# Router logits from unscaled rows, the first gather between products, and another layout of the expert blocks

## The chip, the core and the metric

The kernel runs on one core of one Trainium2 chip. The metric is the time of one execution in device microseconds (us). A profiled execution gives the trace from which rows are shown; its engines are TensorE (PE, with its weight loads as PEld), VectorE (DVE), ScalarE (ACT), GpSimd (POOL) and SyncE (SP), which issues most DMA transfers.

## The reference, cut to what matters

A block of a model over 256 tokens of width 1024. First a mixer (retention and dilated attention, conditioned by adaptive shift and scale), then a mixture of experts over 32 experts, then two more blocks (gMLP or block attention, memory heads, feed-forward). The change lies at the passage from the mixer to the experts:

```python
x = x + gt_a[:, None, :] * (merged @ w_o[l])
h = modulate(rms_norm(x, g_ffn[l]), sh_f, sc_f)     # rms_norm(x)*g*(1+sc) + sh
x = x + gt_f[:, None, :] * moe(h, w_router[l], b_router[l], w_mlp1[l], b_mlp1[l], w_mlp2[l], b_mlp2[l])

# moe: top 4 of 32 experts for each token
logits = (xf @ w_router + b_router).astype(jnp.float32)
top_val, top_idx = lax.top_k(logits, TOP_K)
gates = jax.nn.softmax(top_val, axis=-1)
# each expert: u = xb @ w1[e] + b1[e]; clamped SwiGLU; a @ w2[e] + b2[e], weighted by the gate and added up
```

## The kernel before, in words

One core, all 256 tokens in two row blocks of 128 (`tb`). Weights come through a class `Weights`: a plan lists every weight block in the order of use, `load_next` issues the next DMA on SP, and a block is issued only when the buffer that it goes to has been read by all users of its last content. `in_turn` keeps the issues in the order of the plan.

Up to the expert stage, blocks of 1 MB (`raw`, six buffers) are split by ACT and DVE into a high and a low part (`parts`), and each product is three PE products. The last of these is the output projection `wo` in two column halves (`gemm_nat`, L358 to L392; the branch `wo` of the loop at L825 to L847). Behind each half DVE adds the residual into `x`, ACT squares it with a running sum for the norm, and DVE multiplies by the scale `late["ss"][:, 1]` into `h2`.

Then the routing (L874 to L939), at high priority. For each row block: `rsqrt` by Newton steps on DVE; `h2` is scaled by it and the shift `late["ss"][:, 0]` is added (L897, two halves); eight PE transposes, copied by ACT into `h2T`; 8 products with the router's weights give logits with experts on partitions (L909); ACT adds the bias, PE transposes back (L914). Then DVE's top-8 search, the choice matrix `oh` and its sum `pick` (L916 to L921); three products with a triangular and an all-one matrix give each token's rank in its expert (L923 to L925), `R` (L928). Gates `G`, the overflow flag `novi` (L944 to L951) and the transposed gates `GT` (L958) follow. A copy `h2c` of the scaled rows stays for the gather.

The gather of a pair of experts (L986 to L998): a matrix `ohg` that compares ranks with slot numbers (DVE), and 16 products that pick and transpose the rows of `h2c` into `hg` (64 slots per expert), in four quarters `d0`, each emptied by an ACT copy. All four quarters of pair 0 stand ahead of the first chunk.

The expert stage runs over `jobs`: `chunk(p)` (first weights of pair p, u in four PSUM banks, transposed back, SwiGLU into `apk`) and `second(p)` (second weights, the spread back to tokens), in the order c0, c1, h0, c2, h1, ... Each of the 16 first weights of a chunk is one plan entry of 1 MB; two are loaded by one 2 MB DMA into a turning place. There are eight places, taken in turn: `big0` to `big5` in the pool `upper`, where `raw` and `parts` were, `middle` and `lower` below it. Entries 12 to 15, used in the last quarter of chunk 0, are one-off 1 MB blocks in places of the lasting pool `pa`: x1, x2, reth, retl. The place x1 holds `u` (`us_`) afterwards. `chunk` also issues the next pair's gather, a quarter ahead of each quarter of its own products. The instructions of each engine run in the order that the scheduler fixes from priorities and a simulated time.

After the last pair the turning places are given back, and buffers for the next stage open there, with a place `kvp` for keys and values of the memory heads.

## Time and profile before

| | us |
|---|---|
| median of three timed runs | 1926.49 |
| lowest and highest | 1925.88, 1928.82 |
| profiled execution | 1928.28 |
| its span, first to last instruction | 1926.6 |
| PE busy | 1841.6 (96%) |
| DVE busy | 803.5 (42%) |
| ACT busy | 536.6 (28%) |

The mean granted clock of TensorE is 0.984. A busy time is a count over the whole span and says little of one stage; the rows below are of the passage and of the stage behind it. In a timeline a row can merge several instructions of one kind: start, length from the first start to the last end, and their number behind the x; the brackets give idle time ahead of the first and what ended it. Matmuls are pipelined, so that the ends of neighbours overlap. A float32 product appears as two instructions, a transpose as one.

### The profile page before, as it was taken

What the parts mean: (1) busy time and instruction counts of PE and PEld (TensorE: products, weight loads), DVE (VectorE), ACT (ScalarE), POOL (GpSimd) and SP (SyncE); (2) the same over time, 40 slices, a digit from 0 to 9 for tenths busy, and PEclk for the clock granted to TensorE, in tenths of its full rate; (3) what the DMA queues carried; (4) which work ended last, traced back from release to release, by engine and by line L of the source; (5) the groups of instructions that cost most, each with busy time, mean ns of one, the idle gap of its engine ahead of it and who ended that gap; (6) DMA issues with size and microseconds to landing.
All of it is one profiled execution on the core that took longest, in us unless ns stands there. A gap on an engine that the chain in (4) does not pass through costs nothing. (4 is left out here: it accounts for less than half of the span.)

```text
span 1926.6 us, 23931 instructions
## 1 busy us (share of the span) xinstructions
PE 1841.6 (96%) x10132; PEld 1212.7 (63%) x10132; DVE 803.5 (42%) x1283; ACT 536.6 (28%) x792; POOL 2.6 (0%) x7
## 2 busy tenths in 40 slices
PE   7999999899999999998999899899999999999998
PEld 6899987543344434333333344238889998879997
DVE  5787477422221212221112212028564457565445
ACT  3545454210000000000000000005544445645443
POOL 0000000000000000000000000000000000000000
PEclk9999999999999999999999999999999999999999
DMA  9777476999999999999999999998455555326550
GB/s 359 254 261 249 151 257 229 372 404 416 427 426 427 427 427 427 426 428 427 427 427 427 427 426 427 424 370 294 142 180 190 179 193 176 111 97 225 181 175 23
DMA packets 160403, 593.05 MB, mean 308 GB/s; under 512 B 7643, under 2 KB 92214, under 8 KB 134690
## 3 DMA queue, kind: packets, MB, share of 16 engines
q1 hardware_dynamic: 154008, 583.25, 77.4%
q10 hardware_dynamic: 6282, 8.21, 1.4%
q8 instruction: 81, 1.33, 0.3%
q14 instruction: 32, 0.26, 0.0%
HBM read 590.37 MB, written 1.07 MB: 307 GB/s over the span
## 5 line engine op out<-in xcount | busy, mean ns | idle before, releaser
L1028 PE MATMUL bank_a<-big,hg 128*64 128x512 f32 x2016 | 478.3, 604 | 17.0 <-DMA big<-in_w_mlp 16.9
L197 DVE TENSOR_TENSOR wlo<-raw,whi 128x1024 fp32r<-128x1024 f32 x286 | 345.4, 1222 | 252.7 <-ACT whi L196 251.7
L196 ACT ACTIVATE whi<-raw 128x1024 fp32r<-128x1024 f32 x286 | 298.2, 1058 | 346.9 <-issue 101.0
L1028 PEld LDWEIGHTS bank_a<-big,hg 128*64 128x64 f32 x2016 | 146.5, 139 | 304.1 <-issue 269.4
L1028 PE MATMUL bank_b<-big,apk 128*64 128x512 f32 x928 | 223.6, 617 | 20.7 <-DMA big<-in_w_mlp 20.7
L400 PE MATMUL bank_b<-xh,wlo 128*128 128x256 f32 x640 | 181.1, 283 | 0.0
L398 PE MATMUL bank_b<-xh,whi 128*128 128x256 f32 x640 | 181.1, 283 | 0.0
L399 PE MATMUL bank_b<-xl,whi 128*128 128x256 f32 x640 | 181.0, 283 | 0.0
L1028 PEld LDWEIGHTS bank_b<-big,apk 128*64 128x64 f32 x928 | 84.1, 141 | 148.5 <-issue 93.4
L1050 DVE COPY us<-bank_a 128x512 f32<-128x512 f32 x32 | 22.1, 692 | 345.9 <-PE bank_a L1028 345.9
L398 PEld LDWEIGHTS bank_b<-xh,whi 128*128 128x128 f32 x640 | 122.7, 192 | 0.7
L399 PEld LDWEIGHTS bank_b<-xl,whi 128*128 128x128 f32 x640 | 122.6, 192 | 0.7
L400 PEld LDWEIGHTS bank_b<-xh,wlo 128*128 128x128 f32 x640 | 122.7, 192 | 0.0
L352 ACT ACTIVATE us<-bank_a 128x512 f32<-128x512 f32 x32 | 19.1, 597 | 328.9 <-PE bank_a L1028 328.9
L1086 DVE TENSOR_TENSOR y<-bank_b,gtf 128x512 f32<-128x512 f32 x32 | 22.1, 692 | 201.6 <-PE bank_b L1028 200.1
L352 ACT ACTIVATE spread<-bank_b 128x256 f32<-128x256 f32 x16 | 6.1, 384 | 299.2 <-PE bank_b L1096 299.2
L997 PEld LDWEIGHTS bank_b<-ohg,h2c 128*128 128x128 f32 x512 | 66.1, 203 | 23.0 <-issue 21.1
L997 PE MATMUL bank_b<-ohg,h2c 128*128 128x128 f32 x512 | 72.7, 294 | 0.0
L1499 PE MATMUL bank_a<-wlo,ah 128*128 128x512 f32 x176 | 69.8, 396 | 0.0
L1500 PE MATMUL bank_a<-whi,al 128*128 128x512 f32 x176 | 69.7, 396 | 0.0
L1498 PE MATMUL bank_a<-whi,ah 128*128 128x512 f32 x176 | 69.7, 396 | 0.0
L352 ACT ACTIVATE hg<-bank_b 128x256 f32<-128x256 f32 x64 | 24.6, 384 | 149.2 <-PE bank_b L997 149.2
(382 smaller groups left out, 2735.2 us busy)
## 6 DMA issues: line engine op xcount, KB each, us to landing
big<-in_w_mlp SPq DMA_DIRECT2D x184, 2048.0 KB, 27.0
raw<-in_w_ffn_in SPq DMA_DIRECT2D x44, 1024.0 KB, 5.1
raw<-in_w_in SPq DMA_DIRECT2D x38, 1024.0 KB, 7.5
raw<-in_w_ada SPq DMA_DIRECT2D x24, 1024.0 KB, 6.6
raw<-in_w_ffn_out SPq DMA_DIRECT2D x22, 1024.0 KB, 4.9
raw<-in_w_mlp SPq DMA_DIRECT2D x16, 1024.0 KB, 14.7
raw<-in_b_w_in SPq DMA_DIRECT2D x10, 1024.0 KB, 5.2
raw<-in_w_mix_out SPq DMA_DIRECT2D x8, 1024.0 KB, 5.2
```

Of the source, the lines that this page charges most:

```text
L196: self.nc.scalar.activation(hi, w, AF.Copy)
L197: self.nc.vector.tensor_tensor(lo, w, hi.bitcast(F32), OP.subtract)
L352: return S.activation(o, i, AF.Copy, **kw)
L398: PE.matmul(v[:, m], hi[:, k, ms], xh[:, k], start=k == 0, stop=False)
L399: PE.matmul(v[:, m], hi[:, k, ms], xl[:, k], start=False, stop=False)
L400: PE.matmul(v[:, m], lo[:, k, ms], xh[:, k], start=False, stop=k == 7)
L997: PE.matmul(b[:, n], h2c[:, tb, c0:c0 + 255:2], ohs[p_][:, tb], start=tb == 0, stop=tb == 1)
L1028: last[:] = [PE.matmul(out[at], st, w, start=start, stop=stop)]
L1050: V.tensor_copy(us[:, c + 1], u[c + 1])
L1498: PE.matmul(ops[tb, h], ah[:, k, ts], hi[:, k, hs], start=n + k == 0, stop=False)
L1499: PE.matmul(ops[tb, h], ah[:, k, ts], lo[:, k, hs], start=False, stop=False)
L1500: PE.matmul(ops[tb, h], al[:, k, ts], hi[:, k, hs], start=False, stop=n + k == 11)
```

## The change

- The router's logits are taken from rows that carry only the factor `late["ss"][:, 1]`, not the norm and not the shift. The norm `rs` multiplies the logits afterwards (one DVE instruction with the bias), tokens on partitions. The shift's part of the logits is put into the bias ahead: 16 one-row transposes of the shift into columns `shc`, and 8 products, at the head of the branch `wo`. The gathered rows get the shift when `hg` is written (ACT for pair 0, DVE for the others).
- Three of four transposes' groups and the first row block's products stand directly behind the projection's last product (`latest`); the rest behind these. The second norm waits for the first block's `pick`. The comparison matrix of pair 0 is one instruction behind `R`, and the gates wait for it.
- Of pair 0's gather one quarter stands ahead of chunk 0, the others between its products; the gather of pair 1 stands behind each quarter's products. Overflow, gate transposes, biases and spread of pair 0 come after chunk 0.
- Blocks: eight turning places, now `mid` in the lasting pool, six in `upper`, one in `lower`. One-off blocks in reth, retl, x2 and x1 (entries 12 to 15 in this order; 12, 13 and the first 2 MB into `mid` can be asked for ahead of `upper`). The last two turning entries are loaded alone.
- The lasting `mid` holds qT, kT, eT and g_ffn pieces before, kv, gv and junk after the experts. Shift and scale move from reth to x1. The expert biases load on POOL's queue.

```diff
@@ load_next
-        if i in self.doubles:
+        if i in self.doubles or i in self.lone:
...
+            if i in self.lone:
+                self.load(i, t)
@@ load_free
-                h, size, n = (self.history["big"], 2, len(self.bigs)) if i in self.doubles else \
-                    (self.history["raw"], 1, self.nraw)
-                if len(h) >= n and h[-n] + size > self.taken:
+                h, n = (self.history["big"], len(self.bigs)) if i in self.doubles | self.lone else \
+                    (self.history["raw"], self.nraw)
+                if len(h) >= n and h[-n] + (2 if h[-n] in self.doubles else 1) > self.taken:
@@ ada_late_step
-            late["ss"] = pa.tile([P, 2, D], F32, name="ss", tag="reth")
+            late["ss"] = pa.tile([P, 2, D], F32, name="ss", tag="x1")
@@ branch wo, h == 0
+                wr = small(P, 8, 32)
+                nc.scalar.dma_start(wr, A["w_router"][0].rearrange("(k p) e -> p k e", p=P))
+                br = small(P, 32)
+                nc.scalar.dma_start(br, A["b_router"].to_broadcast([P, 32]))
+                shc = keep.tile([P, 2, 8], F32, name="shc")
+                b = bank("b")
+                for k in range(8):
+                    PE.transpose(b[:, k:k + 1], late["ss"][:1, 0, k * P:(k + 1) * P], ident[:1, :1])
+                    d0 = k // 2 * 256 + k % 2
+                    PE.transpose(b[:, 8 + k:9 + k], late["ss"][:1, 0, d0:d0 + 255:2], ident[:1, :1])
+                copy_s(shc.rearrange("p a k -> p (a k)"), b[:, :16])
+                b = bank("b")
+                for k in range(8):
+                    PE.matmul(b[:, :32], shc[:, 0, k:k + 1].to_broadcast([P, P]), wr[:, k], start=k == 0, stop=k == 7)
+                V.tensor_tensor(br, br, b[:, :32], OP.add)
@@ expert blocks
-    W.bigs = [(upper, f"big{i}") for i in range(6)]
-    W.load_early(first_b + 12, pa.tile([P, 2048], F32, name="raw", tag="x1"))
-    W.load_early(first_b + 13, pa.tile([P, 2048], F32, name="raw", tag="x2"))
-    for _ in range(6):
+    W.bigs = [(pa, "mid")] + [(upper, f"big{i}") for i in range(6)]
+    W.lone = {first_b + 370, first_b + 371}
+    W.load_early(first_b + 12, pa.tile([P, 2048], F32, name="raw", tag="reth"))
+    W.load_early(first_b + 13, pa.tile([P, 2048], F32, name="raw", tag="retl"))
+    W.load_next()
+    W.load_early(first_b + 14, pa.tile([P, 2048], F32, name="raw", tag="x2"))
+    for _ in range(5):
         W.load_next()
...
-    W.bigs += [(middle, "big6"), (lower, "big7")]
+    W.bigs.append((lower, "big6"))
+    W.load_early(first_b + 15, pa.tile([P, 2048], F32, name="raw", tag="x1"))
@@ routing
-            scaled = V.scalar_tensor_tensor(h2[:, tb, hs], h2[:, tb, hs], rs, late["ss"][:, 0, hs], OP.mult, OP.add)
...
+        with after(latest[0]):
+            for tb, h in ((0, 0), (0, 1), (1, 0)):
+                blocks(tb, h)
+            dotted = dots(0)
+        with after(dotted):
+            copied = blocks(1, 1)
+            dots(1)
+        for tb in range(2):
+            if tb:
+                with after(picked):
+                    rs.append(rsqrt(ss2[:, 1, 1:], 1.0 / D, ss2[:, 1, :1], 1))
+            V.scalar_tensor_tensor(lg[:, tb], lts[tb][:, :32], rs[tb], br, OP.mult, OP.add)
...
+        routed = V.tensor_tensor(ohs[0], con("slots")[:, None, None, :SLOTS].to_broadcast([P, 2, 2, SLOTS]),
+                                 R[:, :, :2, None].to_broadcast([P, 2, 2, SLOTS]), OP.is_equal)
+        with after(copied):
+            for tb in range(2):
+                copy_s(h2c[:, tb], h2[:, tb], scale=rs[tb])
+    with after(routed):
+        V.tensor_tensor(gates, mx[:, :, :4], mx[:, :, :1].to_broadcast([P, 2, 4]), OP.subtract)
@@ gather
-        copy_s(hg[:, p_ % 2, :, d0:d0 + 2], b.rearrange("p d e s -> p e d s"))
+        if p_ == 0:
+            for n in range(2):
+                S.activation(hg[:, 0, :, d0 + n], b[:, n], AF.Identity, bias=shc[:, 1, d0 + n:d0 + n + 1])
+            return
+        V.tensor_tensor(hg[:, p_ % 2, :, d0:d0 + 2].rearrange("p e d s -> p d e s"), b,
+                        shc[:, 1, d0:d0 + 2, None, None].to_broadcast([P, 2, 2, SLOTS]), OP.add)
-        for d in range(0, 8, 2):
-            gather(0, d)
+        gather(0, 0)
@@ chunk
-            if ahead is not None:
+            if p_ == 0 and k < 6:
+                gather(0, k + 2)
+            if ahead is not None and p_:
                 gather(ahead, k)
...
+            if p_ == 0:
+                with after(*last):
+                    gather(ahead, k)
@@ jobs
-            spread_pair(p_)
+            if p_:
+                spread_pair(p_)
             chunk(p_, p_ + 1 if p_ < 15 else None)
+            if p_ == 0:
+                overflow()
+                spread_pair(p_)
@@ behind the experts
-    kv = kv_[0]
+    mid = pa.tile([P, 4096], F32, name="kv", tag="mid")
+    kv = mid[:, :2048].rearrange("p (n i b t) -> p n i b t", n=2, i=2, b=2)
```

## Rows read from the trace of the kernel before

**Rows 1.** Page, part 2 (GB/s in 40 slices) and part 6 (us to landing).
```profile
GB/s 359 254 261 249 151 257 229 372 404 416 427 426 427 427 427 427 426 428 427 427 427 427 427 426 427 424 370 294 142 180 190 179 193 176 111 97 225 181 175 23
...
big<-in_w_mlp SPq DMA_DIRECT2D x184, 2048.0 KB, 27.0
```

**Rows 2.** Windows, expert stage: PE, PEld, DVE, ACT, POOL busy (count), clock, DMA share, GB/s.
```profile
600.00:800.00 200.00, 189.77 (x862) 79.09 (x860) 41.68 (x72) 14.78 (x27) 0.00 (x0) 0.97 1.01 427
```

**Rows 3.** Windows with the two holes of the stream.
```profile
412.00:414.00 2.00, 2.00 (x13) 0.58 (x8) 0.61 (x1) 0.00 (x0) 0.00 (x0) 1.00 0.70 295
414.00:416.00 2.00, 2.00 (x12) 1.15 (x9) 0.00 (x0) 0.00 (x0) 0.00 (x0) 1.00 0.72 156
...
470.00:480.00 10.00, 10.00 (x54) 4.85 (x52) 0.99 (x5) 0.77 (x2) 0.00 (x0) 1.00 0.96 375
```

**Rows 4.** Timeline: SP's expert loads, and DVE's last reading of the g_ffn piece.
```profile
306.35 19.32 SPq L133 DMA_DIRECT2D raw<-in_w_mlp  x2
...
316.88 0.69 DVE L630 SCALAR_TENSOR_TENSOR ss<-ss,gff 128x512 f32<-128x512 f32 x1 [0.99 <-ACT ss L352]
...
328.82 10.75 SPq L133 DMA_DIRECT2D big<-in_w_mlp  x3
...
359.24 0.42 SPq L133 DMA_DIRECT2D big<-in_w_mlp  x1
...
377.08 222.92 SPq L133 DMA_DIRECT2D big<-in_w_mlp  x47
...
390.82 24.55 SPq L133 DMA_DIRECT2D big<-in_w_mlp  x4
```

**Rows 5.** Timeline of PE, from the projection's end to the first chunk.
```profile
350.06 1.29 PE L900 MATMUL bank_b<-cm,h 128*128 128x128 f32 x8
351.37 1.94 PE L909 MATMUL bank_b<-h2T,rt 128*32 128x128 f32 x16
...
362.99 0.61 PE L958 MATMUL bank_b<-cm,G 128*32 128x128 f32 x2
363.44 6.60 PE L997 MATMUL bank_b<-ohg,h2c 128*128 128x128 f32 x32
```

**Rows 6.** Windows of the projection.
```profile
320.00:325.00 5.00, 5.00 (x24) 4.14 (x23) 2.19 (x2) 2.50 (x3) 0.00 (x0) 1.00 0.01 2
325.00:330.00 5.00, 4.18 (x27) 3.40 (x26) 4.99 (x8) 2.22 (x4) 0.00 (x0) 1.00 0.68 223
```

**Rows 7.** Timeline of DVE in the routing, second row block.
```profile
352.69 0.21 DVE L431 TENSOR_SCALAR rs_z<-rt 128x1 f32<-128x1 f32 x1
...
354.09 1.41 DVE L897 SCALAR_TENSOR_TENSOR h<-h,rs_y,ss 128x512 f32<-128x512 f32 x2
...
359.52 0.20 DVE L916 MAX8 rt<-bank_b 128x8 f32<-128x32 f32 x1 [0.51 <-PE bank_b L914]
...
360.60 0.37 DVE L921 TENSOR_REDUCE rt<-rt 128x32 f32<-128x128 f32 x1
...
361.69 0.22 DVE L928 SCALAR_TENSOR_TENSOR R<-bank_b,rt 128x64 f32<-128x64 f32 x1
...
363.10 0.49 DVE L991 TENSOR_TENSOR ohg<-cm,R 128x128 f32<-128x128 f32 x2
```

**Rows 8.** Timeline at the turn from the first chunk to the second.
```profile
390.62 7.04 PE L1028 MATMUL bank_a<-raw,hg 128*64 128x512 f32 x32
...
395.16 0.60 ACT L352 ACTIVATE us<-bank_a 128x512 f32<-128x512 f32 x1 [24.70 <-PE bank_a L1028]
...
398.89 3.93 PE L997 MATMUL bank_b<-ohg,h2c 128*128 128x128 f32 x32
```

**Rows 9.** Windows of one us: busy of PE first, granted clock third from the end.
```profile
362.00:363.00 1.00, 0.13 (x3) 0.10 (x3) 0.93 (x5) 0.00 (x0) 0.00 (x0) 0.68 1.06 442
...
365.00:366.00 1.00, 1.00 (x7) 1.00 (x7) 0.00 (x0) 0.02 (x1) 0.00 (x0) 0.50 0.99 426
...
369.00:370.00 1.00, 1.00 (x10) 0.88 (x9) 0.00 (x0) 0.35 (x1) 0.00 (x0) 0.90 1.07 459
```

More of the change, by code (lines that the diff above doesn't have):

```diff
@@ L721, in body @@
     pt = ea.enter_context(tc.tile_pool(name="pt", bufs=1, reuse_waits="tile"))
+    mid = pa.tile([P, 4096], F32, name="mid", tag="mid")
+    eTs = [mid[:, 1024 + i * 384:1024 + (i + 1) * 384] for i in range(2)]
     M = {}
@@ L795, in gate, with small @@
         return s_
+    rt, rt_used = None, [4]
+    def small(p, *shape):
+        n = int(np.prod(shape))
+        v = rt[:p, rt_used[0]:rt_used[0] + n]
+        rt_used[0] += n
+        if len(shape) == 2:
+            v = v.rearrange("p (a b) -> p a b", a=shape[0])
+        if len(shape) == 3:
+            v = v.rearrange("p (a b c) -> p a b c", a=shape[0], b=shape[1])
+        return v
     for st_ in stage:
@@ L883, in body, with blocks @@
     ixf = small(P, 2, 8)
+    lg = small(P, 2, 32)
     oh = small(P, 2, 4, 32)
     pick = small(P, 2, 32)
+    ohs = {0: keep.tile([P, 2, 2, SLOTS], F32, name="ohg0", tag="GT")}
     ones = con("ones")
-    hi_prio = ExitStack()
-    hi_prio.enter_context(tc.high_priority())
-    with after(late["sq", 1]):
-        S.activation(small(P, 1), ss2[:, 0, :1], AF.Exp)
+    G = keep.tile([P, 2, 32], F32, name="G")
+    R = keep.tile([P, 2, 32], F32, name="R")
     tss = [slice(0, P), slice(P, T)]
-    copied = None
-    for tb in range(2):
-        rs = rsqrt(ss2[:, tb, 1:], 1.0 / D, ss2[:, tb, :1], 1)
-        for h in range(2):
-            hs = slice(h * 512, h * 512 + 512)
-            scaled = V.scalar_tensor_tensor(h2[:, tb, hs], h2[:, tb, hs], rs, late["ss"][:, 0, hs], OP.mult, OP.add)
+    with tc.high_priority():
+        S.activation(small(P, 1), late["sq0"], AF.Exp)
+        rs = [rsqrt(ss2[:, 0, 1:], 1.0 / D, ss2[:, 0, :1], 1)]
+        lts = [bank("a") for _ in range(2)]
+        def blocks(tb, h):
             b = bank("b").rearrange("p (k t) -> p k t", k=4)
@@ L900, in body @@
                 PE.transpose(b[:, k], h2[:, tb, (4 * h + k) * P:(4 * h + k + 1) * P], ident)
-            c_ = copy_s(h2T[:, 4 * h:4 * h + 4, tss[tb]], b)
-            copied = copied if h else c_
-        if tb:
-            for t_, after_ in ((0, (late["sq", 1], scaled)), (1, (scaled, copied))):
-                with after(*after_):
-                    copy_s(h2c[:, t_], h2[:, t_])
-        lt = bank("b")
-        for k in range(8):
-            PE.matmul(lt[:32, :P], wr[:, k], h2T[:, k, tss[tb]], start=k == 0, stop=k == 7)
@@ L922, in body @@
-    rb = bank("b")
-    PE.matmul(rb[:, :32], con("before"), pick[:, 0], start=True, stop=True)
-    PE.matmul(rb[:, 32:64], ones, pick[:, 0], start=True, stop=False)
-    PE.matmul(rb[:, 32:64], con("before"), pick[:, 1], start=False, stop=True)
-    G = keep.tile([P, 2, 32], F32, name="G")
-    R = keep.tile([P, 2, 32], F32, name="R")
-    V.scalar_tensor_tensor(R, rb[:, :64].rearrange("p (b e) -> p b e", b=2), 1.0, pick, OP.add, OP.mult)
-    dump("h2", h2)
-    gates = small(P, 2, 4)
-    V.tensor_tensor(gates, mx[:, :, :4], mx[:, :, :1].to_broadcast([P, 2, 4]), OP.subtract)
@@ L932, in body @@
-    exped = S.activation(gates, gates, AF.Exp)
-    gl = small(P, 2)
-    V.reduce_sum(gl, gates, AX.X)
-    V.reciprocal(gl, gl)
-    V.tensor_tensor(gates, gates, gl[:, :, None].to_broadcast([P, 2, 4]), OP.mult)
-    for tb in range(2):
-        V.tensor_tensor(oh[:, tb], oh[:, tb], gates[:, tb, :, None].to_broadcast([P, 4, 32]), OP.mult)
-        V.reduce_sum(G[:, tb], oh[:, tb].rearrange("p k e -> p e k"), AX.X)
-    hi_prio.close()
+            return copy_s(h2T[:, 4 * h:4 * h + 4, tss[tb]], b)
@@ new lines, in body @@
+        rb = bank("b")
+        PE.matmul(rb[:, :32], con("before"), pick[:, 0], start=True, stop=True)
+        PE.matmul(rb[:, 32:64], ones, pick[:, 0], start=True, stop=False)
+        PE.matmul(rb[:, 32:64], con("before"), pick[:, 1], start=False, stop=True)
+        V.scalar_tensor_tensor(R, rb[:, :64].rearrange("p (b e) -> p b e", b=2), 1.0, pick, OP.add, OP.mult)
+        routed = V.tensor_tensor(ohs[0], con("slots")[:, None, None, :SLOTS].to_broadcast([P, 2, 2, SLOTS]),
+                                 R[:, :, :2, None].to_broadcast([P, 2, 2, SLOTS]), OP.is_equal)
@@ L983, in body @@
     us_ = pa.tile([P, 4, 512], F32, name="us", tag="x1")
-    spread, ohs = {}, {}
+    spread = {}
     def gather(p_, d0):
-        if d0 == 0:
+        if d0 == 0 and p_:
             ohs[p_] = pe.tile([P, 2, 2, SLOTS], F32, name="ohg")
@@ L1266, in body @@
         nc.gpsimd.memset(q, 0.0)
-    junk = pc.tile([P, D], mybir.dt.bfloat16, name="junk")
+    junk = mid[:, 3584:].bitcast(mybir.dt.bfloat16)
     def normalize(dst, src, st, n, gb):
```

135 lines of the change are left out of this document (63 added, 72 removed).

## The prediction

> **What bounds the kernel now.** I read the slices of the page first: from about 380 to 1250 us the core moves 404 to 428 GB/s and nothing else in the page is as flat [rows 1]. The windows of that stretch say the same more sharply: DMA share 1.01 at 427 GB/s, while PE counts 190 of 200 us [rows 2]. This stage streams 184 blocks of 2048 KB [rows 1] and, by the plan, 16 of 1024 KB of expert weights, 402.7 MB, which at 427 GB/s is 943 us. Whatever moves the end of this stage must move the start of the stream or close a hole in it.
>
> So I looked for holes. There are two behind the start: 412 to 416 us, where the rate falls to 295 and 156, and a small one around 470 to 480 at 375 [rows 3]. In bytes the first is (427-295) x 2 + (427-156) x 2, about 0.8 MB or 1.9 us, the second (427-375) x 10 = 0.5 MB or 1.2 us. The queue's own timeline shows why: two blocks are asked for at 390.82, and the next not before about 414 (the last two of the four that the row merges), since their buffers come free only when the second chunk's first products are through [rows 4]. Products of the first chunk's last quarter free no turning place, because they read the four one-off blocks. Thus **the stream's place after 414 us is set by PE**, not by how early the first blocks were asked for. From the gather at 363.44 on, PE is without a gap, up to beyond that release and through the next one near 474 [rows 3, 5]. After that DMA is the later of the two and stays so. Ahead of 350 us PE is full as well: the output projection runs at 5.00 of 5.00 us per window, with one hole of 0.82 us in 325 to 330 [rows 6]. Between them lies the only stretch in which PE waits: the routing, from 350.0 to 363.4, and after it a gather that runs at half clock.
>
> The forecast is therefore one sum along PE: from the end of the projection to the second chunk's first release, plus what is added ahead of it.
>
> **Part by part.**
>
> *Earlier blocks (reth, retl, mid, x2 ahead of the upper pool; scale and shift in x1).* Today one 1 MB block is asked for at 306.35 and the next about 19 us later, behind the attention buffer; the first 2 MB block follows at 328.82 [rows 4]. After the change two blocks have a free place at 306, the 2 MB one in the lasting pool when the g_ffn piece is read (317.6, the end of L630 [rows 4]), and x2's at 325 as now. That is 5 MB ahead of the upper pool in place of 2: 3 MB, or 7.4 us of stream. But the eight turning places and four one-off blocks still hold 20 MB, and the fifteenth turning block still waits for the second chunk's first products. The lead is spent as a longer hole before 414 us. I count it as 0; its upper worth, 7.4 us, is a rival. On SP's queue these loads stand behind the projection's weights and ahead of expert weights alone. The last two single blocks and the new overlay at the stage's end delay a few 1 MB requests by one quarter chunk (about 7 us) while four to five blocks (27.0 us from issue to landing [rows 1]) are queued: 0. The memories that move into the lasting pool (qT, kT, eT, kv, gv, junk) keep their readers and writers in the same order: 0, with up to 1 us either way.
>
> *Shift columns, new work ahead of the projection.* 16 transposes of a one-row strip, one copy, 8 products (two instructions each, as the sixteen of L909 are for eight) and one add. PE has no cover here but the 0.82 us hole. Price of the transposes, from the nearest rows: at most that of full 128 x 128 ones, eight in 1.29 us, 0.16 each, 2.6 in all; at least a third of that, 0.9, as strips are small. The 16 product instructions: 1.94 us [rows 5]. Sum 2.8 to 4.5, less the hole: **+2.0 to +3.7**, or at best 0, if the order finds more holes. I take +2.7. The Trainium skill ("TensorE: Matmul & The Clock Gate", Part 2, step-by-step) says that loading the stationary operand takes time by its columns and not by its rows, which speaks against the change: a strip of one row by 128 columns would cost what a full block does, and the sum would be +3.7 in place of +2.7. No row here shows a one-row load.
>
> *The routing chain.* Before, from the last product of the projection (350.0, where L900 begins) to the first gather product (363.44): 13.4 us [rows 5]. In it the second row block waits for its own scale (L431 at 352.69) before two scalings of 1.41 us at 354.09; then four transposes and copies, the products, a bias on ACT, a transpose back, and the top-4 chain from 359.52 [rows 7]. After: the unscaled rows need neither scale nor shift, so 12 transposes can start at 350.0 (1.5 us), 8 products of the first row block end near +3.5, the last 4 transposes and the copy follow, and the second block's logits are in PSUM near +6.0. On DVE the first block's chain (L916 to L921, 1.45 us, and a new 0.25 us scaling) ends near +5.3; then, by the order written out, the second scale (1.4, from L431 to L897) at +6.7; then 0.25 + 1.45 again to +8.4; from there to R as now, 0.72 (360.97 to 361.69), and R itself 0.22, to +9.3; one comparison of 128 x 256 in place of two of 128 x 128 (0.49 together), now directly behind R instead of 1.4 us later behind gates and overflow [rows 7]. First gather near **+9.9**: -3.5 us. Waits added: the comparison no longer queues behind the gate arithmetic, which now waits for it; nobody needs the gates before the first chunk ends. The two row copies h2c wait for the second scale on ACT and are through ahead of the gather.
>
> *Gather between products.* The gather of the first pair is 32 instructions: 6.60 us ahead of the first product, at half clock [rows 5], against 3.93 at full clock later [rows 8]. Now one quarter stands ahead and the rest, with the next pair's, between the products. PE does the same instructions on the same gapless path, so moving them gains nothing by itself: the half clock then falls on products instead. From the row, the clock is 0.68 in 362 to 363, 0.50 after that and 0.90 in 369 to 370, after PE had been busy for 0.13 us of a whole one [rows 9]: 6.6 us at half speed, some 3 us lost. After the change the quiet stretch before the gather is 4 us again. I take the same loss, with -2.9 (no fall) to +1.7 (half clock for 10 us) as ends, and lean by -0.4, as the quiet is shorter by one half microsecond.
>
> *Work that comes out of the shadow.* The overflow count and the gate transposes (L958 alone is 0.61 us of PE [rows 5]) stood inside the chain's waits; now they follow the first chunk: +0.6. The biases go from SP's queue to POOL's, where nothing else is queued for hundreds of us; on SP three issues vanish after 359.24 with nothing behind them until 377.08 [rows 4]: 0. Gathers emptied by DVE instead of ACT: neither is near its bound in that stage: 0.
>
> *The turn between the chunks.* The x1 block is now the last of the four one-off blocks and is read by the very last product of the first chunk; the copy of u goes to x1. Today it starts at 395.16, 2.5 us before the last products end (390.62 + 7.04 = 397.66) [rows 8]. After, it starts at the end. PE then has the bias transposes, overflow and spread (about 2.1 us) and the second chunk's products to do. I take +0.3, with 0 to 4.5 as ends.
>
> Sum: +2.7 - 3.5 - 0.4 + 0.6 + 0.3 = -0.3 us; with the small leaning of the memory moves left at 0, **-0.3 us**. The profiled execution took 1928.28 us (span 1926.6), which gives 1928.0. The median of the three timed runs is 1926.49, 1.8 lower, so on the timed scale **1926.2 us**.
>
> **Rivals.**
> - *The clock stays up or the strips are hidden.* With PE busy through more of the chain, the clock need not fall: -2.9; with the strips in holes of the order, -2.7 more. Either alone stays within 4 us, both give 1926.2 - 5.6 = 1920.6; together with half of one, about 1922. For: PE's quiet is shorter than now. Against: 4 us of it remain, and no holes are seen before 350. The Trainium skill ("TensorE: Matmul & The Clock Gate", Part 1) says that the throttled state is the default and activity releases it; the rows agree [rows 9], and no run here shows yet what this quiet does.
> - *The lead of 3 MB reaches the end.* If the second chunk's release came 7 us earlier, the stream would keep its lead: 1926.2 - 7.4 = 1918.8. Against: the release is PE's, by the sum above.
> - *Slower: the turn.* If PE's order leaves the transposes of u at the head while the copies, which start 2.5 us later, and DVE's four additions run one after the other (in the row they are spread over 6 us with products between), PE loses up to 4.5 us before the second release: 1926.2 + 4.2 = 1930.4, and beyond with the full price of the strips (1931.4). It decides from some 4 us of stall on.
> - *The change doesn't do what it says.* If the scheduler puts the whole gather ahead of the products as now, PE's total is the same, and the time too: 1926.
>
> **How the numbers follow.** What a measurement of this kernel can tell from no change is about 0.2%, 3.9 us. Forecast (within 3.9 us of before): 0.54; the turn: 0.16; clock and strips: 0.17; the lead: 0.08; the scheduler's undoing: 0.05, same time. Faster by over 0.2%: 0.17 + 0.08 = 0.25. Same: 0.54 + 0.05 = 0.59. Slower: 0.16. Range: 1921.0 to 1931.0, leaving out the lead and the ends of the rivals beyond it.
>
> **What would show it.** In the changed profile: two 1 MB and one 2 MB expert block asked for before 320 us; the hole of DMA before the second chunk's release near 414 grown from 2 to about 9 us; the projection's end moved from 350.0 to about 352.7; first gather about 10 us behind that; the second chunk's first release within 3 us of 414. If that release moves by more than 4 us, the forecast is wrong by as much, and the step is the one whose row moved: strips, chain, clock or turn. If it doesn't move but the time does, the cause lies behind 1300 us, in a place I set at 0.

## The result, and where the profile after differs

The changed kernel took 1942.55 us (median of 4 runs, 1939.38 to 1947.76) against 1927.65 for the kernel before on the same chip: a ratio of 1.0079, 95% interval 1.0066 to 1.0092. It is **slower by 0.8%**, 11.6 us above the upper end of the forecast's range. The profiled execution took 1939.72 us (span 1938.0 against 1926.6), one of the two faster of its four; the other two took 1945 and 1948.

Where 11.3 us arise, as far as one trace of each kernel tells, is read from how much later the same event comes in the trace after than in the trace before:

| event | before, us | after, us | shift | gained or lost since the row above |
|---|---|---|---|---|
| last 1 MB block of `w_o` asked for | 305.89 | 309.18 | +3.3 | +3.3 |
| first product of the output projection | 326.99 | 337.93 | +10.9 | +7.6 |
| its last product ends | 349.99 | 360.89 | +10.9 | 0 |
| first gather | 363.44 | 371.94 | +8.5 | -2.4 |
| 25th block of 2 MB asked for | 456.73 | 466.52 | +9.8 | +1.3 |
| last expert product ends | 1297.70 | 1309.12 | +11.4 | +1.6 |
| first block of `w_ffn_in` asked for | 1357.4 | 1370.9 | +13.5 | +2.1 |
| last product of PE | 1918.28 | 1929.59 | +11.3 | -2.2 |

The largest loss lies where I had put +2.7: ahead of the projection. The first product is no like mark in the two traces: before, six products stand between the first eight of the 16 transposes of `m1` (the rows that the projection reads) and the next, and PE waits 0.82 us there; after, all 16 come first. The projection's end is a like mark, and gives the same +7.6 since the `w_o` block. The timeline of PE after (start, duration, engine, line), answering [rows 5]:

```profile
329.51 0.22 PE L856 MATMUL bank_b<-cm,ss 1*128 1x1 f32 x1
...
330.85 0.25 PE L858 MATMUL bank_b<-cm,ss 1*128 1x1 f32 x1
331.38 3.43 PE L862 MATMUL bank_b<-rt,shc 128*128 128x32 f32 x16 [0.27 <-ACT shc L356]
334.62 3.65 PE L565 MATMUL bank_b<-cm,m 128*128 128x128 f32 x16
337.93 0.71 PE L370 MATMUL bank_a<-whi,hh 128*128 128x512 f32 x1
...
360.73 1.47 PE L923 MATMUL bank_b<-cm,h 128*128 128x128 f32 x12
362.04 2.84 PE L928 MATMUL bank_a<-rt,h2T 128*128 128x32 f32 x24
...
366.74 1.89 PE L928 MATMUL bank_a<-rt,h2T 128*128 128x32 f32 x8
...
371.94 3.75 PE L1027 MATMUL bank_b<-ohg,h2c 128*128 128x128 f32 x16 [0.87 <-DVE rt L961]
```

The 16 one-row transposes are cheap, 1.6 us; the 16 product instructions behind them (L862) take 3.43 us, where 24 of the same shape take 2.84 at 362.04 (the 16 of [rows 5], 1.94, from which I had the price, have another shape), and then the 16 transposes of `m1` (L565), older work, take 3.65. The windows of this stretch (busy of PE, PEld, DVE, ACT, POOL, then granted clock, DMA share, GB/s) say why: 0.50 is 1.2 GHz, and PE has no pause in it. In [rows 6] all is at 2.4.

```profile
330.00:332.00 2.00, 1.73 (x17) 1.64 (x16) 2.00 (x4) 0.91 (x2) 0.00 (x0) 0.90 0.71 172
332.00:338.00 6.00, 6.00 (x31) 6.00 (x30) 2.27 (x4) 1.74 (x3) 0.00 (x0) 0.50 1.00 374
338.00:340.00 2.00, 2.00 (x10) 1.64 (x9) 1.38 (x2) 0.66 (x2) 0.00 (x0) 0.89 1.00 426
```

SP's expert loads, answering [rows 4], came as the diff says: two at 309.64 (before: one), the 2 MB one of `mid` at 321.59. The second chunk's first release went from 414.20 to 421.50, and the hole ahead of it grew as forecast (198 and 291 GB/s below, 329 and 431 before):

```profile
309.64 1.07 SPq L133 DMA_DIRECT2D raw<-in_w_mlp  x2
321.59 0.33 SPq L133 DMA_DIRECT2D big<-in_w_mlp  x1
...
421.50 10.97 SPq L133 DMA_DIRECT2D big<-in_w_mlp  x4
```

```profile
410.00:420.00 10.00, 10.00 (x58) 4.91 (x58) 5.12 (x11) 2.15 (x4) 0.00 (x0) 1.00 0.47 198
420.00:430.00 10.00, 10.00 (x50) 3.89 (x47) 2.66 (x8) 1.91 (x3) 0.00 (x0) 1.00 0.77 291
```

Three smaller losses stood at 0 or nowhere in my sum: +3.3 ahead of 306 us, +1.6 at the end of the expert stage, +2.1 behind it; and the last stage runs *faster* than before.

### The profile page after: what moved, and what is told of

Its sections match the earlier page's. It is cut to its first block, busy times and chain, and to the rows that moved or that the text cites. A ratio compares the mean times of both kernels' runs of the same rounds, so it can differ in the third digit from the quotient of the medians.

```text
span 1938.0 us, 23994 instructions
## 1 busy us (share of the span) xinstructions
PE 1846.8 (95%) x10162; PEld 1212.1 (63%) x10162; DVE 824.7 (43%) x1341; ACT 514.8 (27%) x735; POOL 4.2 (0%) x10
## 5 line engine op out<-in xcount | busy, mean ns | idle before, releaser
L1055 PE MATMUL bank_b<-big,apk 128*64 128x512 f32 x928 | 219.0, 606 | 20.0 <-DMA big<-in_w_mlp 20.0
L1055 PEld LDWEIGHTS bank_b<-big,apk 128*64 128x64 f32 x928 | 78.3, 139 | 149.1 <-issue 100.7
L1032 DVE TENSOR_TENSOR hg<-bank_b,shc 128x256 f32<-128x256 f32 x60 | 25.4, 423 | 103.6 <-PE bank_b L1027 103.6
```

What stands on the lines that cost most here:

```text
L1032: V.tensor_tensor(hg[:, p_ % 2, :, d0:d0 + 2].rearrange("p e d s -> p d e s"), b, shc[:, 1, d0:d0 + 2, None, None].to_broadcast([P, 2, 2, ...
L1055: last[:] = [PE.matmul(out[at], st, w, start=start, stop=stop)]
```

## Experiments

Sixteen kernels. Where an expectation speaks of the eighth, eleventh or fourteenth experiment, it counts otherwise than here: they are 10, 6 and 12. Shifts are against the trace before. One thing blurs them: near 50 us the clock falls for longer in some executions than in others, which moves all that follows by up to 4 us (at 60 us the traces lie between -1.8 and +4.3 of the one before). The same window in the trace before, and in that of the fourteenth kernel, which has the same work there (clock third from the end):

```profile
50.00:55.00 5.00, 5.00 (x17) 3.28 (x17) 4.88 (x7) 5.00 (x8) 0.00 (x0) 0.82 1.04 385
```

```profile
50.00:55.00 5.00, 5.00 (x11) 2.71 (x11) 4.77 (x11) 4.41 (x7) 0.00 (x0) 0.50 1.04 385
```

So I read differences of shifts within a trace, and medians for whole times; a median of five or six executions can still hold more of the one kind than of the other.

### The strips

**1. Without strips.**

```diff
-                for k in range(8):
-                    PE.transpose(b[:, k:k + 1], late["ss"][:1, 0, k * P:(k + 1) * P], ident[:1, :1])
...
+                V.memset(shc, 0.0)
```

> The changed kernel with the shift's 16 one-row transposes and 8 products left out ahead of the output projection (the shift columns are set to zero, so the shift is missing from the logits and from the gathered rows). Clock theory (the strips bring TensorE from 2.4 to 1.2 GHz and cost some 8 us with it): no granted clock under 1.00 between 325 and 350 us of the trace, the projection ends at 352 to 353 instead of 360.7, and the time is 1934, with 1932 to 1936. Rival one, strips cost only their own work of 2.5 to 3 us at full clock and the fall of the clock comes from something else: 1940. Rival two, the memory that moved in the attention stage makes the loss: projection still ends beyond 357, time 1939 to 1942.

Measured: 1938.4 us, clock 1.00 in all of 320 to 360, projection's end at +6.0 where the `w_o` block is at +4.4, thus +1.6 in place of +7.6 since that block. The strips cost 6.0 us there, and no fall of the clock is left. Other experts are chosen without the shift, so later stages aren't read. The time fell by 4, not 8: the rest of the loss is elsewhere.

**2. Strips alone, on the kernel before.**

```diff
+                wr2 = rt[:, 1200:1456].rearrange("p (a b) -> p a b", a=8)
+                shc = keep.tile([P, 2, 8], F32, name="shc")
...
+                    PE.matmul(b[:, :32], shc[:, 0, k:k + 1].to_broadcast([P, P]), wr2[:, k], start=k == 0, stop=k == 7)
```

> The kernel before with nothing but the strips' work added ahead of the output projection (16 one-row transposes, one copy, 8 products, one add, and the load of the router weights a second time); the results go unused, the routing is the old one. Clock theory: the granted clock falls to 0.50 for some 7 us near 326 to 333, the projection ends at 357 to 358 instead of 350.0, and the time is 1935 to 1936. Rival, work only: projection end 352.7, time 1930.4, clock at 1.00. Rival two (memory moves make the loss): as rival one, since memory is as before.

Measured: 1928.23 us, ratio 0.9998 (0.9989 to 1.0008). By the time alone strips would be free. The trace says otherwise: from the `w_o` block (+0.7) to the projection's end (+8.0) the shift grows by 7.4, much of it at half clock (part belongs to the slower step of the products, told below), and it is still +6.3 at the last expert product. In the last stage it melts to +1.0.

```profile
330.00:340.00 10.00, 10.00 (x43) 8.94 (x44) 2.95 (x5) 3.01 (x5) 0.00 (x0) 0.68 0.67 255
```

Some other effect gives 5.3 us behind the last expert product, in a kernel whose last stage I had not touched.

**3. Strips spread.** The 16 transposes, still in one piece, behind modulation step 7 in the attention stage; products one at a time between the projection's.

```diff
+                if fill:
+                    fill.pop(0)()
...
+                    fill.append(lambda k=k: PE.matmul(late["bb"][:, :32], shc[:, 0, k:k + 1].to_broadcast([P, P]), wr[:, k],
```

> The changed kernel with the same strips in other places: the 16 one-row transposes right behind the modulation step that fills the shift, in the attention stage, and the 8 products one at a time between the dense products of the first half of the output projection. Clock theory: the clock stays at 1.00 through projection, the strips cost 2 to 3 us of work, projection ends near 355, time 1935 to 1938. Rival, work and not clock: the same instructions cost the same wherever they stand, time 1941 to 1943. If the 16 transposes alone bring the clock down where they now stand, a stretch at 0.50 shows up there and the gain is only half: 1938 to 1940.

Measured: 1941.14 us, by the median in the rival's range; the trace, of the fastest of five executions (1936.62), speaks for the clock theory. The granted clock is 1.00 from 320 to 360, the `m1` transposes take 1.03 + 0.60 + 0.60 = 2.23 instead of 3.65, each pair of product instructions 0.30:

```profile
330.56 1.03 PE L567 MATMUL bank_b<-cm,m 128*128 128x128 f32 x8
333.92 0.60 PE L567 MATMUL bank_b<-cm,m 128*128 128x128 f32 x4
334.83 0.60 PE L567 MATMUL bank_b<-cm,m 128*128 128x128 f32 x4
335.49 0.30 PE L866 MATMUL bank_b<-rt,shc 128*128 128x32 f32 x2
```

The transposes now stand at 297.95 to 299.54 us, among large products, and leave the clock at 1.00 too:

```profile
295.00:300.00 5.00, 5.00 (x31) 4.07 (x30) 5.00 (x9) 1.25 (x2) 0.00 (x0) 1.00 0.64 210
```

They thus lie ahead of the `w_o` block, and I count from an older mark, the last product with `reth` (288.28 us before). From there to the projection's end the shift grows by 5.1 here (+2.7 to +7.8), without strips by 1.6, in the changed kernel by 7.6: **spread, the strips cost 3.5 us, in one piece 6.0**. The difference goes with the clock. Which part of the row of transposes, wait, narrow products and the transposes of `m1` behind them brings it down is not shown, but the 16 one-row transposes alone did not. Of the 2.5 us won by the projection's end the median shows 1.4.

### Memory and the order of blocks

**4. Old routing, new memory.** The change with the routing and gather of before, no strips.

```diff
-        if p_ == 0:
-            for n in range(2):
-                S.activation(hg[:, 0, :, d0 + n], b[:, n], AF.Identity, bias=shc[:, 1, d0 + n:d0 + n + 1])
...
+        copy_s(hg[:, p_ % 2, :, d0:d0 + 2], b.rearrange("p d e s -> p e d s"))
```

> The changed kernel with the whole routing and gather of the kernel before (rows scaled and shifted first, whole first gather ahead of the products, no strips), but with the new turning places, early blocks and moved memories. If memory and early blocks cost nothing, as I forecast: 1927.6 within 2 us, projection end at 350 to 351. If the memory moves in the attention stage make some 3 us of the loss: projection end near 353, time 1930.5 to 1931.5. If the lead of early blocks is worth something: below 1924.

Measured: 1937.19 us, ratio 1.0053. None of the three: the shift is +0.5 at the 25th block, so attention and early blocks are nearly free, and the loss comes late: +3.5 at the last expert product, +8.8 from 1401 us on. SP's timeline at the stage's end (`mem` is the memory heads' input, `gfin` the final gain), before and then this kernel:

```profile
1242.01 7.67 SPq L133 DMA_DIRECT2D raw<-in_w_mlp  x6
1255.79 0.38 SPq L1156 DMA_DIRECT2D mem<-in_mem  x1
```

```profile
1234.79 7.19 SPq L133 DMA_DIRECT2D big<-in_w_mlp  x3
1256.41 0.38 SPq L1163 DMA_DIRECT2D mem<-in_mem  x1
1258.54 0.34 SPq L1192 DMA_DIRECT2D gfin<-in_g_final  x1
1259.21 33.03 SPq L133 DMA_DIRECT2D raw<-in_w_mlp  x12
```

The single blocks are asked for 17 us later, behind `mem`, and the stream has a hole of (427 - 304) x 10 and (427 - 388) x 10, 1.6 MB or 3.8 us:

```profile
1250.00:1260.00 10.00, 10.00 (x52) 4.44 (x50) 4.33 (x8) 1.19 (x2) 0.00 (x0) 1.00 0.76 304
1260.00:1270.00 10.00, 6.55 (x28) 1.77 (x24) 1.91 (x3) 1.06 (x1) 0.00 (x0) 1.00 1.00 388
1270.00:1280.00 10.00, 8.61 (x28) 2.70 (x29) 0.00 (x0) 0.00 (x0) 0.00 (x0) 0.66 0.98 380
```

The kernel before has a hole of the same size, (427 - 266) x 10, some 25 us later:

```profile
1280.00:1290.00 10.00, 8.78 (x32) 2.61 (x32) 0.00 (x0) 0.00 (x0) 0.00 (x0) 0.83 0.75 266
```

So the hole alone doesn't tell the loss. What grew are PE's waits for single blocks (us in total, number, longest; 1240 to 1320 us, before and then this kernel), 2.0 us more, and the stretch at half clock behind them, 0.66 against 0.83 of 10 us, by estimate 1.7 us; the shift grew by 3.0:

```profile
PE bank_b L1028 <- DMA raw<-in_w_mlp: 4.3, 2, 3.1
PE bank_b L1037 <- DMA raw<-in_w_mlp: 6.3, 3, 3.9
```

**5. `mem` behind the single blocks**, on the changed kernel.

```diff
+            with tc.issue_after(W.loads[-1].ins):
-            mem_load()
+                mem_load()
...
```

> The changed kernel with the loads of mem and of the final gain made to wait for the first six 1 MB expert blocks of the last pair, which is the order that the kernel before had on the queue (in the changed one the two stand ahead of them and mem waits for the last gather, so the first 1 MB block is asked for at 1268.5 where before asked at 1242.0). Theory, stage end: the hole in the stream behind the last 2 MB block closes, the last expert product ends 3 to 4 us earlier relative to the first chunk's releases (shift against before +7.5 to +8 at the last expert product instead of +11.4), time 1938 to 1939, or 1935 if the memory stage behind it gains too. Rival, the order on the queue does not matter because PE is the later one there: 1942.

Measured: 1943.91 us, ratio 1.0084 (1.0071 to 1.0097). The rival, and 2 us above it: first single block at 1256.5 (changed kernel 1268.5), yet between the 25th block (+11.3) and the last expert product (+13.4) still 2.1.

**6. No single blocks ahead of the last stage**, on the fourth kernel.

```diff
-    W.doubles = {first_b + i for i in range(0, 370, 2) if not 12 <= i < 16}
-    W.lone = {first_b + 370, first_b + 371}
+    W.doubles = {first_b + i for i in range(0, 372, 2) if not 12 <= i < 16}
```

> The fourth kernel (old routing, new memory) with the last two expert blocks ahead of the last stage loaded as one 2 MB block again, not as two single 1 MB blocks in two turning places. Theory, single blocks: they push the places of the last six blocks one turn on, so mem and the first 1 MB blocks come late; undone, the first 1 MB block is asked for within 3 us of 1242, the last expert product ends at 1298 (shift 0 to +0.5 instead of +3.5), time 1930 to 1933. Rival, the loss comes from mid as a turning place and from the last stage's tiles that lie in it: shift at the last expert product stays +3 to +4, time 1937.

Measured: 1933.6 us, 3.6 below the fourth kernel, but not by the way I expected: the first single expert block still goes out behind `mem`, and the shift grows by 4.0 from the 25th block (+4.5) to the last expert product (+8.5). The gain lies behind that product, by 1401 us: +1.1 in place of +5.3.

**7. Both.**

```diff
-    W.lone = {first_b + 370, first_b + 371}
...
+            with tc.issue_after(W.loads[-1].ins):
```

> Old routing, new memory, the last two blocks as one 2 MB block, and the loads of mem and final gain behind the first six 1 MB blocks. Theory, order on the queue: with both undone the first 1 MB block is asked for at the same shift as the last 2 MB block, the last expert product's shift falls by 3 to 4 us against the eleventh experiment, time 1929 to 1930.5. Rival, the lasting turning place itself moves the stage's end, whatever the order: 1933 to 1934, as the eleventh.

Measured: 1938.81 us, 4.8 us above the rival's range and 8.3 above the theory's (two of six executions took 1934.1 and 1934.7, the others 1938.3 to 1939.7, the traced one among them); from the 25th block (+4.6) to the last expert product (+8.5) again 3.9, and behind it +2.6. The rival holds for the stage's end, order isn't the cause there. SP's timeline (the row of ten merges issues at 1248.00, 1248.38, 1254.85 and on):

```profile
1241.12 0.80 SPq L133 DMA_DIRECT2D big<-in_w_mlp  x2
1248.00 31.94 SPq L133 DMA_DIRECT2D raw<-in_w_mlp  x10
1280.00 0.45 SPq L1162 DMA_DIRECT2D mem<-in_mem  x1
```

The third single block comes at 1254.85, before at 1243.12: less the 4.6, 7 us late. By the code, `mid` takes the first turn of eight, so every other place comes one 2 MB block later in the last round, and it is on those places that the single blocks lie; no run moves the places alone, so this step is read from code and rows. The hole then is at 1270 (300 GB/s), and PE waits 5.72 us for a block, then runs at half clock (0.74 in the window); before it waited 3.12 and 1.23:

```profile
1270.00:1280.00 10.00, 9.80 (x43) 3.31 (x38) 1.20 (x2) 0.00 (x0) 0.00 (x0) 1.00 0.78 300
1290.00:1300.00 10.00, 4.28 (x12) 1.07 (x11) 0.00 (x0) 0.00 (x0) 0.00 (x0) 0.74 1.03 386
```

```profile
1296.67 6.55 PE L1036 MATMUL bank_b<-raw,apk 128*64 128x512 f32 x18 [5.72 <-DMA raw<-in_w_mlp]
```

**8. New one-off blocks, own turning places and memories.**

```diff
-    W.load_early(first_b + 12, pa.tile([P, 2048], F32, name="raw", tag="x1"))
...
+    W.load_early(first_b + 12, pa.tile([P, 2048], F32, name="raw", tag="reth"))
+    W.load_early(first_b + 13, pa.tile([P, 2048], F32, name="raw", tag="retl"))
...
```

> The kernel before with the early and one-off blocks of the change (12 and 13 in reth and retl, 14 in x2, 15 in x1; scale and shift in x1, biases on the other queue), but with its own turning places and memories (no turning place in the lasting pool, nothing moved into it) and its own routing. Theory, the lasting turning place: the +8.8 of the fourth kernel at the end vanishes altogether, time 1926 to 1928, with two 1 MB expert blocks asked for near 307. Rival, the one-off blocks make the loss: shifts of +3.5 at the last expert product and +8.8 at the end stay, time 1935 to 1937.

Measured: 1929.76 us, 1.8 above the forecast, ratio 1.0011 (1.0001 to 1.0020); -0.2 at the last expert product, +0.1 at the end. So, by what is left over between this kernel and the fourth, **the turning place in the lasting pool and what comes with it (single blocks, moved memories) cost the 8 to 9 us** of the fourth kernel; the one-off blocks cost 1.4 us by the medians, 0.2 to 3.9 by the interval. The blocks were early here too, and the single ones at the end as before:

```profile
304.57 19.31 SPq L133 DMA_DIRECT2D raw<-in_w_mlp  x3
...
1239.83 9.54 SPq L133 DMA_DIRECT2D raw<-in_w_mlp  x6
```

### The step of a product

Nothing so far explains +3.3 ahead of 306 us or the gains in the last stage of the second kernel. The rows that differ are old ones: the same products, of the same shape (`ah` and `al` are the high and low parts of the feed-forward's activations in the last stage). Groups by line (busy, mean ns of one) in 270 to 320 us and 1440 to 1520 us, before and then after:

```profile
L364 PE MATMUL bank_a<-wlo,reth 128*128 128x512 f32 x16 | 6.2, 389 | 0.0
...
L1499 PE MATMUL bank_a<-wlo,ah 128*128 128x512 f32 x40 | 15.9, 396 | 0.0
```

```profile
L370 PE MATMUL bank_a<-wlo,reth 128*128 128x512 f32 x16 | 6.3, 397 | 0.0
...
L1541 PE MATMUL bank_a<-wlo,ah 128*128 128x512 f32 x32 | 12.5, 390 | 0.0
```

Products overlap; from start to start the median is 227 ns before and 234 after in the first stretch, 234 and 229 in the second (means over the products with `ah` and `al`). Ahead of 360 us 720 products of this shape run, the projection's 96 among them. In the compiled kernels the tiles of rows (`hh`, `hl`, `reth`, `xh`, `mixh`) start at byte 480 modulo 512 before, 32 in the second kernel, 64 after, since the lasting small tiles had grown by 64 and 96 bytes; the weight parts `whi` and `wlo` always at 480.

**9. Two unused tiles in the changed kernel** bring the rows' tiles and `ah`, `al` to the weight parts' place modulo 256.

```diff
     over = keep.tile([P, 2, 32], F32, name="over")
+    keep.tile([P, 40], F32, name="pad")
...
+    pc.tile([P, 40], F32, name="pad")
```

> The changed kernel with nothing but two unused tiles of 160 bytes per partition: one at the end of the lasting small tiles, one ahead of the last stage's tiles. They move the rows' and activations' tiles (hh, hl, xh, mixh and so on) from 96 bytes behind the weight parts' place (counted modulo 256) to the same place as the weight parts, as in the kernel before, and the last stage's ah and al from 192 behind to the same. Placement theory: the step of a 128x512 product is set by where its two operands lie in the on-chip memory; it falls from 234 to 227 ns ahead of the projection's end, which comes some 4 us earlier (356 to 357 instead of 360.7), and from 229 to 227 in the feed-forward of the last stage; time 1937 to 1939. Rival, the step is a state of the run or of the chip: steps stay at 234 and 229, time 1942.

Measured: 1938.93 us, 3.6 less than the changed kernel. From start to start 227 ns in every stretch, first and last. Its trace is of the slowest of six executions (1941.72), so only growth is read: from 60 us to the `w_o` block 0.6 us (+1.4 to +2.0), where the changed kernel has 2.7 (+0.6 to +3.3) and the first and fifth 2.6; from there to the projection's end 5.9 against 7.6. The placement thus cost some 2 us and 1.7 us. In 270 to 320 us:

```profile
L370 PE MATMUL bank_a<-wlo,reth 128*128 128x512 f32 x16 | 6.2, 389 | 0.0
```

**10. One unused tile in the kernel before**, for `ah` and `al` alone.

```diff
...
+    pc.tile([P, 104], F32, name="pad")
```

> The kernel before with one unused tile of 416 bytes per partition ahead of the last stage's tiles, so that ah and al lie at the same place modulo 512 as the weight parts; nothing else. Placement theory: the step of the feed-forward's 528 products falls from 234 to 227 ns, 3.7 us in all, time 1923 to 1924. Rival, step is a run's state: 1927, step 234.

Measured: 1924.08 us, ratio 0.9986 (0.9977 to 0.9994), as forecast within 0.1 us. Only the products with `ah` and `al` changed:

```profile
L1500 PE MATMUL bank_a<-wlo,ah 128*128 128x512 f32 x38 | 14.8, 390 | 0.0
```

**11 and 12. Other distances in the kernel before.**

```diff
+    keep.tile([P, 16], F32, name="pad")
...
+    pc.tile([P, 88], F32, name="pad")
```

> The kernel before with two unused tiles: 64 bytes per partition in the lasting small tiles (the rows' tiles then lie 64 bytes behind the weight parts, counted modulo 256) and 352 ahead of the last stage's tiles (ah and al at the weight parts' place). Placement theory, from the steps of the second and eighth experiments: 128x512 products of the rows at 233 instead of 227 ns, 128x256 products at 117 instead of 120, the feed-forward's 528 products at 227 instead of 234: ahead of 360 us about even, in the last stage -6 to -9, time 1918 to 1921. Rival, the 128x256 steps of the second experiment came from its strips or its run: 1924 as the eighth.

> As the one ahead, with 32 bytes in place of 64 (rows' tiles 32 behind the weight parts; ah and al again at the same place). Placement theory: 128x512 between 227 and 233 ns, so about 230, 128x256 between 114 and 120; time 1919 to 1924. It tells whether the step follows the distance smoothly. Rival: it jumps, and one of the two kinds of product is as in the kernel before.

Measured: 1919.64 us (ratio 0.9953, 0.9939 to 0.9967) with 64, and 1919.61 (0.9950, 0.9936 to 0.9965) with 32 (8 and 96 floats). **Both beat the kernel before and the changed one, with no instruction changed.** The step doesn't follow the distance smoothly: at 32 as at 64 the 128x512 products take 232 to 234 ns (234 in the last of the sixteen kernels, at 32), the 128x256 ones 117 to 118 instead of 120. In 1440 to 1520 us, before and then with 32:

```profile
L398 PE MATMUL bank_b<-xh,whi 128*128 128x256 f32 x146 | 41.3, 283 | 0.0
...
L398 PE MATMUL bank_b<-xh,whi 128*128 128x256 f32 x154 | 42.9, 279 | 0.0
...
L1501 PE MATMUL bank_a<-wlo,ah 128*128 128x512 f32 x39 | 15.2, 390 | 0.0
```

Windows of the last stage, before and with 32: 2719 and 2770 PE instructions in the same 400 us.

```profile
1440.00:1840.00 400.00, 395.58 (x2719) 360.36 (x2718) 221.44 (x293) 191.47 (x285) 0.00 (x0) 1.00 0.51 170
```

```profile
1440.00:1840.00 400.00, 395.92 (x2770) 362.57 (x2769) 224.62 (x295) 193.32 (x288) 0.00 (x0) 1.00 0.51 172
```

This is also why the second kernel came out even: its strips' columns, 64 bytes in the lasting tiles, sped up the last stage by about what the strips had cost (its 128x256 products there take 118 ns, before 120).

### Together

**13. Strips spread, both unused tiles, `mem` behind the single blocks.**

```diff
+    keep.tile([P, 40], F32, name="pad")
...
+            with tc.issue_after(W.loads[-1].ins):
```

> Three edits together on the changed kernel: strips spread as in the third experiment, both unused tiles as in the first of this set, and the six blocks ahead of mem. If the causes add up: strips -1.4 (measured), placement -4 to -5, stage end -3.5 to -7, so 1928 to 1933. If one of them is only a shift of the same wait, the sum falls short by that term.

Measured: 1934.9 us, ratio 1.0038; 7.7 of the 15 us are back. It misses the forecast by 1.9 us; the order doesn't mend the stage's end (5 and 7).

**14 to 16. The new routing without the side costs:** one-off blocks, logits and gather of the change on the memories and turning places of before; then the transposes off PE; then that with the placement of the twelfth.

```diff
+                nc.gpsimd.tensor_tensor(dg, v, ident[:, None, None, :].to_broadcast([P, 4, 2, P]), OP.mult)
+                V.reduce_sum(late["shc"][:, a], dg.rearrange("p k n q -> p (k n) q"), AX.X)
```

> The kernel before with the change's one-off blocks, its unscaled logits and its gather between products, strips spread, but with the turning places and memories of before and the rows' tiles kept at the weight parts' place (160 unused bytes). Theory, side costs: what is left of the loss is the strips' own work, some 2.7 us, and the new chain gives 2.2 of it back: projection end +2.5 to +3.5, second release of the stream (block 24 of the 2 MB ones) +0.5 to +1.5, time 1927 to 1929.5. Rival, the new routing costs more behind 450 us too (gathers emptied on another engine): 1931 or more.

> As the one ahead, with the 16 one-row transposes taken off TensorE: a product with the unit matrix on the idle engine and a sum on VectorE make the shift columns in the attention stage; 8 products stay, one at a time in the projection. Theory: projection end +1 to +2, second release -1 to 0, time 1925.5 to 1927.5. Rival, VectorE's sums (2 of some 1.1 us) delay the splitting of weights in the attention stage as much as the transposes cost: as the one ahead, 1927 to 1929.

> As the one ahead, with the placement of the fourteenth experiment (rows' tiles 32 bytes behind the weight parts, ah and al at their place). If placement and routing add up: 1926.5 less 8 to 9, so 1917.5 to 1919; if the routing gives nothing, 1919.6 as the fourteenth.

Measured: 1930.71 us (ratio 1.0014, 1.0005 to 1.0023), 1928.14 (0.9997, 0.9988 to 1.0006) and 1920.45 (0.9962, 0.9949 to 0.9975). The first is 1 us above its range, the second 0.6. Without strips the routing is worth nothing measurable, and with the placement it ends level with the twelfth kernel, which has the old routing. PE in the second of these:

```profile
352.01 1.47 PE L923 MATMUL bank_b<-cm,h 128*128 128x128 f32 x12
...
357.57 1.06 PE L928 MATMUL bank_a<-rt,h2T 128*128 128x32 f32 x8
...
361.94 3.75 PE L1029 MATMUL bank_b<-ohg,h2c 128*128 128x128 f32 x16 [0.87 <-DVE rt L961]
```

From the first transposes behind the projection to the first gather 9.9 us, the forecast's figure to the tenth. The shift is +2.2 at the projection's end (the 8 products), -1.5 at the first gather, and +0.1 again at the 25th block.

## Why the prediction was wrong

The direction was wrong (59% on no change), and the time lies outside the range. By its steps:

- *What bounds the kernel.* Right: PE sets the second chunk's first release. That it "doesn't move by more than 4 us" was the test that I named; it moved by 7.3, and the step whose row moved was the strips.
- *Strips, +2.7.* **The term that was mis-sized**: +7.6 in the table, 6.0 of it theirs (1 and 3). As work at full clock they cost 3.5, inside my 2.0 to 3.7; the hole of 0.82 us that I had taken off was still there (PE 9.18 of 10 us in 330 to 340, third kernel). The other 2.5 are what I didn't ask for: what they do to the clock of the work around them. I had looked for half clock where PE waits; here PE had only a wait of 0.27 us, between one-row transposes and products of 32 columns, and fell to 1.2 GHz for 6 us; 16 transposes of `m1` paid with them. The rule of the Trainium skill on loading by columns ("TensorE: Matmul & The Clock Gate", Part 2, step-by-step) nearly holds: from start to start the one-row strips took 0.09 us each (329.51 to 330.85 in 15 steps), 12 full blocks 0.11 each (360.73 to 362.04). My price of a full block, 0.16, was what was too high.
- *Routing chain, -3.5.* Right in itself: 9.9 us (15). After it was 11.2 (360.73 to 371.94), and the gain 2.2: the clock fell earlier in the chain, and the second block's 8 product instructions took 1.89 us in place of 1.06.
- *Gather between products, overflow, turn, +0.5 together.* +1.3 after, +1.6 in the fifteenth kernel: a little low. The slower rival, a stall at the turn, didn't occur: PE is 10.00 of 10.00 us busy in 410 to 430.
- *Earlier blocks, 0.* Right within the noise (8): asked for earlier, spent in the hole before the release.
- *Single blocks and the new overlay at the stage's end, 0.* Wrong. The delay of "about 7 us" was right, its cover was not: I took four to five queued blocks of 27 us from the stage's middle, but at its end no further 2 MB blocks follow, and PE waits for single blocks there, 6.1 us in the changed kernel where it waited 4.3 before (1.6 of loss in the table, 3 to 4 in 4, 6 and 7). I should have read the windows behind 1250 us as I read those at 414.
- *Memory moves, 0 within 1.* In the attention stage right (4: +0.9 from 100 us to the `w_o` block). Behind the expert stage wrong: +2.1 after, +5.3 in the fourth kernel. Without the single blocks it was +1.1 (6) and +2.6 (7); by which wait isn't shown, only that PE in the fourth waits 1.98 us for ACT and drops to 0.70 of the clock in 1315 to 1320. The cause of this part stays open.
- *What no step held.* The rows' tiles moved by 96 bytes, which cost some 2 us ahead of the `w_o` block and 1.7 up to the projection's end (9); in the last stage the shift fell by 2.6, from +13.9 at 1418 us to +11.3, with the step of `ah` and `al` down from 234 to 229 ns. Of the +3.3 ahead of 306 us, 0.6 was there at 60 us, from the early clock.

The reading "wrong by the strips" alone would be as wrong as the forecast. Without strips (1) the kernel was still 0.6% slower; undoing memory and placement and spreading the strips (14: +0.14%), or taking the transposes off PE as well (15: -0.03%), brings back the result, within 3.9 us of before, that the sum had.

## What to carry to other kernels

Price small work on TensorE twice: once as instructions, once by what the clock does to the work behind it, and put it between large products. A buffer that joins a rotation can shift the phase of its last round; read the queue at the end of the stage, not in its middle. And before an edit is blamed or praised for under 1%, look whether old, untouched products have kept their step.

## What the runs showed of the hardware

- In these kernels the step of a product changed with where its operands start in the on-chip memory. Rows' tile against weight part, in bytes modulo 256: at 0, 227 ns (128x512) and 120 ns (128x256); at 32 and 64, 232 to 234 and 117 to 118; at 96, 234 and 119 to 120. For 1919.6 against 1928.4 us only unused tiles were added. The weight parts' place never varied, so whether the distance counts or the rows' own place is open.
- TensorE's clock was at 1.2 GHz through a stretch in which PE was busy in 6.00 of 6.00 us. Ahead of its fall stood 16 one-row transposes, a wait of 0.27 us and the first 32-column products. It stayed at 2.4 (1.00 in 295 to 300 and 320 to 360 us) when the transposes, in one piece, and the products, in pairs, stood between large ones.
